# Start addresses of TensorE's operands at multiples of 64 bytes: a hybrid decoder trunk on one core

## The chip, the core and the metric

The kernel runs on one core of a Trainium2 chip. The metric is the device time of one launch in microseconds (us): the median of the kernel before is 1512.21 us over 3 runs (1512.15 to 1514.15).

## The reference

T = 272 tokens (16 learned ones ahead of 256) of D = 1024 features go through two layers in float32. Cut to what is computed:

```python
# layer 0
gate, xr = split(h @ w_in)                    # RG-LRU: 1024 -> 2 x 1344
xc = causal width-4 convolution of xr
r, i = sigmoid(blockdiag(xc) + b)             # 8 blocks of 168
a = exp(-8 r softplus(-lam)); u = sqrt(1 - a*a) * i * xc
hs = linear scan over time of (a, u)
h = LN(alpha h + (hs * gelu(gate)) @ w_out)
h = LN(alpha h + (silu(h @ wg) * (h @ wu)) @ w_ff_out)    # 1024 -> 3584 -> 1024
# layer 1
q, k, v, r, z = split(h @ w_in)               # gated linear attention, 4 heads, chunks of 64
h = LN(alpha h + (LN(attention) * silu(r)) @ w_out)
h = LN(alpha h + sum over the top 2 of 8 experts of gate * swiglu_e(h))   # 1024 -> 3584 -> 1024
out = h without the 16 learned tokens
```

## The kernel before

**Arithmetic.** Each large product is done in three passes of TensorE on operands of the type float32r. Weights and activations are split into a high part and a low part (`split`, line 269: a copy on ScalarE, a subtraction on VectorE), and `mm3` (line 273, matmuls at lines 275 to 277) issues low weight times high activation, high times low, high times high into one PSUM bank.

**Weights.** The class `Weights` streams all weights through SBUF: DMAs of up to 1 MB issued on SyncE's queue (line 97) into nine `raw` buffers (later up to 14), then pieces of 1024 columns split into `whi` on ScalarE (line 127) and `wlo` on VectorE (line 137), six buffers each. A piece is split four ahead of its use.

**Stages, in order of time.** In the trunk (all before the experts) a weight block of 128 x 128 is the stationary operand and one row of the tokens, `xh[:, k]` or `xl[:, k]`, is the moving one: 272 columns, 274 in a few stages (two more columns carry the norm's gain and bias), 256 or 258 where the learned tokens are left out. The stages are `xr` (convolution input, 264 matmuls), `g` (gates, 162), `gb` (gate branch, 264), `ro` (output of the recurrent block, 264), `fg`/`fu` (input of the dense channel mixer, 96 + 1248), `fo` (its output, 672), `z`/`k`/`q` (24 + 96 + 96), `vT` (192), `r` (192) and `go` (output of attention, 72 of 512 columns and 48 of 256). `xr`, `gb`, `fg`/`fu`, `z`, `k`, `q`, `vT` and `r` read `xh` and `xl`, 2472 matmuls in all. `g` and `ro` read `ch` and `cl`, `fo` reads `fh` and `fl`, whose rows are 272 elements apart. In `go` the roles are turned: `xh` and `xl` are stationary (128 columns of a row) and the weights move.

**Experts.** For each of 8 experts and 7 blocks j, `stage_in` (line 1319) does 48 matmuls with the gathered tokens `xe` stationary (128 x 128) and 512 weight columns moving, `stage_tr` (line 1337) transposes the gated product `hb` in four blocks and splits it into `hh` and `hl`, and `stage_out` (line 1351) does 24 matmuls with `hh` and `hl` stationary. That is 56 x 72 = 4032 matmuls of three passes, `pg`, `pu` and `y`.

**Places in SBUF.** Every tile takes a multiple of 32 bytes of each partition. Pools that live to the end lie one behind another from byte 1152 up: `wraw`, `wparts`, `const`, `keep`, `moe`, `late`, `rows`, `moe2`. Pools of the trunk are stacked from byte 229344 down (`side="right"`): `resid` (with `xh`, `xl`), below it `x`, and below that, one after another in time, `rg`, `ffn` and `gla`. A pool's tiles lie in the order of their creation from its lower end. So a tile of 32 bytes moves everything behind it in its own pool, and all pools stacked on that pool. In the allocation of the kernel before, the operands of the large products start here:

| tile | first byte | row pitch (bytes) | start mod 64 | start mod 128 |
|---|---|---|---|---|
| `whi`, `wlo` (all 12 buffers) | 74880 up | 512 or 2048 | 0 | 0 |
| `xh`: row k at 209504 + 1096 k | 209504 | 1096 | 32, 40, 48, 56, 0, 8, 16, 24 | 96, 40, 112, 56, 0, 72, 16, 88 |
| `xl` | 218272 | 1096 | the same | 32, 104, 48, 120, 64, 8, 80, 24 |
| `ch`; `cl` | 142048; 154016 | 1088 | 32 in every row | 96; 32, then alternating |
| `fh`; `fl` | 132160; 162624 | 1088 | 0 in every row | 64 in even rows, 0 in odd rows |
| `xe`, `hh`, `hl` (experts) | 213120 / 204928, 223360, 225408 | 512 | 0 | 0 |
| `x3h`, `x3l` (gathering) | 135648, 143840 | 512 | 32 | 96 |

**Order around the change.** The tokens' rows are written by `split` and by the class `Norm`; the edits touch the tiles alone. `clear` (line 696) fills 512 rows of `yd` in DRAM with zeros, four DMAs on SyncE's queue from the tile `zero`. `cm` (line 641) is a mask of 128 x 128 that GpSimd makes and VectorE copies into `cmask` at once; `tmp2` (lines 729 and 731) is a ring of two buffers for the exponents of the gates. The tiles of `moe`, `late` and `rows` lie where `gla` and `x` were, and each waits for the tiles that it overlaps.

Of the kernel before, what the change touches and what calls it, by code (L numbers as in the profile page):

```python
# [11 lines left out]
F32 = mybir.dt.float32  # L12
F32R = mybir.dt.float32r
# [6 lines left out]
P = 128  # L20
D = 1024
KD = D // P
NM = 16
NX = 256
T = NM + NX
ALPHA = float((2 * 2) ** 0.25)
EPS = 1e-5
TINY = 1e-34
# [157 lines left out]
def trunk_kernel(ctx: ExitStack, tc: tile.TileContext, xT_d, rgp_d, lnT_d, rgin_d, rgg_d, rgout_d,  # L186
                 fin_d, fout_d, bg_d, wup_d, zqk_d, vr_d, go_d, rows_d, rt_d, min_d, mout_d,
                 out, dbg=None):
    nc = tc.nc
# [44 lines left out]
    const = ctx.enter_context(tc.tile_pool(name="const", bufs=1))  # L234
    ps = ctx.enter_context(tc.tile_pool(name="ps", bufs=8, space=PSUM))
    dram = ctx.enter_context(tc.tile_pool(name="dram", bufs=1, space=bass.MemoryType.DRAM))
    yd = dram.tile([2 * NX + P, D], F32, name="yd")
# [15 lines left out]
    one_c = const.tile([P, 1], F32, name="one_c")  # L253
    nc.vector.memset(one_c, 1.0)

    onetri = const.tile([P, 2, P], F32, tag="onetri", name="onetri", bufs=1)
    ones, tri = onetri[:, 0], onetri[:, 1]
    nc.gpsimd.memset(ones, 1.0)
# [10 lines left out]
    def split(dst_h, dst_l, src):  # L269
        nc.scalar.copy(dst_h, src)  # L270
        nc.vector.tensor_sub(dst_l, src, dst_h)
# [6 lines left out]

    res = ExitStack()
    resid = res.enter_context(tc.tile_pool(name="resid", bufs=1, side="right"))  # L280
    xh = resid.tile([P, KD, T + 2], F32R, name="xh")
    xl = resid.tile([P, KD, T + 2], F32R, name="xl")
    nmu = resid.tile([P, T], F32, name="nmu")
    rstd_x = resid.tile([P, T], F32, name="rstd_x")
    lnT = resid.tile([P, 4, KD], F32, name="lnT")
    xs = ExitStack()
    x = xs.enter_context(tc.tile_pool(name="x", bufs=1, side="right")).tile([P, KD, T], F32, name="x")
    for n, (k0, k1) in enumerate(((0, 1), (1, 2), (2, 4), (4, 6), (6, 8))):
        W.limit = n + 1
        W.load()  # L290
        nc.sync.dma_start(x[:, k0:k1], xT_d[:, k0:k1])
        split(xh[:, k0:k1, :T], xl[:, k0:k1, :T], x[:, k0:k1])
    W.limit = len(units)
# [5 lines left out]
    def unfold(dst, pp, pool, name, c0=0):  # L299


        n = T - c0
        gb = pool.tile([P, 2], F32, tag="unfold", name=f"unfold_{name}", bufs=3)
        nc.vector.tensor_copy(gb, pp[:, n:n + 2])
        nc.vector.scalar_tensor_tensor(dst, nmu[:, c0:], gb[:, 0:1], pp[:, :n], op0=ALU.mult, op1=ALU.add)
        nc.vector.tensor_mul(dst, dst, rstd_x[:, c0:])
        return gb[:, 1:2]
# [8 lines left out]
    class Norm:  # L316
# [12 lines left out]
        def add(self, d, y):  # L329
            if d == 0:  # L330
                nc.vector.scalar_tensor_tensor(x[:, 0], x[:, 0], ALPHA, y, op0=ALU.mult, op1=ALU.add)
            else:
# [5 lines left out]
        def center(self):  # L338
# [6 lines left out]
            for k in range(1, KD):  # L345
                nc.vector.scalar_tensor_tensor(x[:, k], x[:, k], ALPHA, c, op0=ALU.mult, op1=ALU.subtract)
            self.square(0)
# [211 lines left out]
    def ffn_in(fs, c1):  # L559
        pps = [bank(f"f{t}{f}") for f in fs for t in "gu"]  # L560
        for k in range(KD):
            for pp in pps:
                mm3(pp[:, :c1], W.take(P), xk(k, 0, c1), k == 0, k == KD - 1)
            if c1 > T and k == 0:
                norm.sums(True)
        return pps
# [9 lines left out]
    fp = fps.enter_context(tc.tile_pool(name="ffn", bufs=1, side="right"))  # L576
    fh = fp.tile([P, NF, T], F32R, name="fh")
    fl = fp.tile([P, NF, T], F32R, name="fl")
    for f in range(NF):
        gt = fp.tile([P, T], F32, tag="gt", name=f"gt{f}", bufs=2)  # L580
        if f < 2:
            up = fp.tile([P, T], F32, tag="gt", name=f"up{f}", bufs=2)
            bg, bu = unfold(gt, first[2 * f], fp, f"fg{f}"), unfold(up, first[2 * f + 1], fp, f"fu{f}")
            nc.scalar.activation(gt, gt, AF.Silu, bias=bg)
            nc.vector.scalar_tensor_tensor(gt, up, bu, gt, op0=ALU.add, op1=ALU.mult)
        else:
            pg, pu = ffn_in((f,), T)
            silu = nc.scalar.activation(gt, pg[:, :T], AF.Silu)
            nc.vector.tensor_mul(gt, gt, pu[:, :T])
        split(fh[:, f], fl[:, f], gt)  # L590
# [47 lines left out]
    gp = ga.enter_context(tc.tile_pool(name="gla", bufs=1, side="right"))  # L638
    wu = gp.tile([P, 512], F32, tag="vm", name="wu", bufs=1)
    nc.sync.dma_start(wu, wup_d)  # L640
    cm = gp.tile([P, P], F32, name="cm")

    zero = gp.tile([P, 256], F32, name="zero")
    nc.gpsimd.memset(zero, 0.0)
    cmask = gp.tile([P, P], U32, name="cmask")
    nc.gpsimd.affine_select(out=cm, in_=ones, pattern=[[1, P]], compare_op=ALU.is_ge, fill=0.0, base=0,
# [47 lines left out]
    nc.gpsimd.memset(rstd_x, 0.0)  # L694

    def clear(a):
        nc.sync.dma_start(yd[a * P:(a + 1) * P].rearrange("p (b c) -> p b c", b=4),
                          zero[:, None, :].broadcast_to([P, 4, 256]))

    side.put([lambda: None] * 6 + [lambda g=g: gate_exp(g) for g in range(H)]  # L700
             + [lambda g=g: gate_log(g) for g in range(H)] + [lambda a=a: clear(a) for a in range(2 * NX // P)])
    for h in range(2, H):
        (pk,), (pq,) = qk((h,), T)
# [52 lines left out]
    def x_rows(i, q):  # L756
        pt = bank(f"xt{i}{q}")
        for k in range(4):
            nc.tensor.transpose(pt[:, k * P:(k + 1) * P], x[:, q * 4 + k, NM + i * P:NM + (i + 1) * P], ident)
        nc.scalar.activation(acc[:, i, q * 512:(q + 1) * 512], pt, AF.Copy, scale=ALPHA)  # L760

# [149 lines left out]
    moe = ctx.enter_context(tc.tile_pool(name="moe", bufs=1, reuse_waits="tile"))  # L911
    x3h = moe.tile([P, 2, D], F32R, name="x3h")
    x3l = moe.tile([P, 2, D], F32R, name="x3l")

    def small(name, shape, dt=F32):
        return moe.tile(shape, dt, name=name)
# [377 lines left out]
    def add_back(n, i):  # L1294
        a = acc[:, i]
        if n == 0:
            nc.vector.scalar_tensor_tensor(a, a, ALPHA, back[0][:, i], op0=ALU.mult, op1=ALU.add)
        else:
# [226 lines left out]
    with tc.If(nmax > P):  # L1525
# [3 lines left out]
        for e in range(NE):  # L1529
# [24 lines left out]
            for j in range(JM):  # L1554
                pg = bank(f"vpg{e}{j}")
                pu = bank(f"vpu{e}{j}")
                for kk in range(4):
                    w = raw_piece(min_d[e, j, kk // 2][:, (kk % 2) * PIECE:(kk % 2 + 1) * PIECE],
                                  f"vwi{e}{j}{kk}")
                    for k2 in range(2):  # L1560
                        k = kk * 2 + k2
                        for s, pp in ((0, pg), (1, pu)):
                            c = k2 * 1024 + s * 512
# [10 lines left out]
                for b, (q, s) in enumerate(out_blocks(e, j)):  # L1574
                    if b % 4 == 0:
                        w = raw_piece(mout_d[e, j][:, b * 512:(b + 4) * 512], f"vwo{e}{j}{b}")
                    c = b % 4 * 512
                    nc.tensor.matmul(py[s], ht[:, q * P:(q + 1) * P], w[:, c:c + 512],
                                     start=(j == 0 and q == 0), stop=(j == JM - 1 and q == 3))
            for s in range(2):  # L1580
                yv = gb.tile([P, 512], F32, tag="xg", name=f"vyv{e}{s}", bufs=4)
                nc.scalar.activation(yv, py[s], AF.Copy, scale=gs)
                for i in range(2):
                    c = slice(s * 512, (s + 1) * 512)
# [91 lines left out]
```

## Time and profile before

| | |
|---|---|
| median of 3 runs | 1512.21 us (1512.15 to 1514.15) |
| the profiled execution's own time | 1512.2 us |
| its span, first to last instruction | 1510.3 us |
| mean granted TensorE clock | 0.997 |
| TensorE busy | 1486.3 us, 98% |
| VectorE, ScalarE busy | 1262.3 us, 84%; 1058.7 us, 70% |

How to read it: TensorE's matmuls overlap, so the time that one takes (some 290 ns at 272 columns) is not the pace. The pace is the time from the start of one matmul to the start of the next, which the timeline gives to 10 ns, and to less over a run of many.

### The profile page before, as it was taken

Reading aid. Unit: us, or ns where it says so; the run is one execution under the profiler, and the core shown is the slowest. Engines: PE = TensorE matmul, PEld = TensorE weight load, DVE = VectorE, ACT = ScalarE, POOL = GpSimd, SP = SyncE. Lnnn points to the kernel's source line nnn. Section 1 sums busy time; section 2 is a strip of 40 time slices with the busy share of each in tenths; the row PEclk is TensorE's granted clock in tenths of the full one; section 3 lists DMA queues with packets and bytes.
Section 4 is the critical chain, followed back from the end, with each engine's and each line's share of the span. In section 5 each row is a group of like instructions: output and inputs, shape, how many; then the busy total and the mean of one; then the engine's idle time right before and its main releaser. Section 6 shows DMA issues by size and latency. Waiting matters only on the chain.

```text
span 1510.3 us, 22283 instructions
## 1 busy us (share of the span) xinstructions
PE 1486.3 (98%) x8393; PEld 1302.8 (86%) x8393; DVE 1262.3 (84%) x1492; ACT 1058.7 (70%) x1369; POOL 116.7 (8%) x151
## 2 busy tenths in 40 slices
PE   9989999999999999999999999999999999999996
PEld 9989999999998888888888888888888888888875
DVE  7699755555796699999998899898899899989897
ACT  6866644444685588878887778777787777777774
POOL 5443000002100000001000000000000000000001
PEclk9999999999999999999999999999999999999998
DMA  9536544445653579999999999999998899999973
GB/s 367 184 134 236 185 178 157 152 166 182 231 186 107 212 274 393 338 337 401 419 376 380 345 393 380 369 391 393 372 379 350 334 379 385 374 371 381 378 250 115
DMA packets 70500, 450.67 MB, mean 298 GB/s; under 512 B 8144, under 2 KB 10480, under 8 KB 22256
## 3 DMA queue, kind: packets, MB, share of 16 engines
q1 hardware_dynamic: 67696, 439.20, 76.7%
q0 software_dynamic: 2688, 9.96, 1.6%
q8 instruction: 68, 1.11, 0.3%
q14 instruction: 48, 0.39, 0.1%
HBM read 441.26 MB, written 7.86 MB: 297 GB/s over the span
## 4 chain that ended last, share of the span: by engine, by line
PE 92%; DVE 4%; ACT 2%; issue 1%; POOL 1%; DMA 0%; SPq 0%; DVEq 0%; ACTq 0%; POOLq 0%
PE pg L276 7%; PE pg L275 7%; PE pg L277 7%; PE y L276 7%; PE pu L276 7%; PE pu L277 7%; PE pu L275 7%; PE y L275 7%; PE y L277 7%; PE fg L276 2%; PE fg L277 2%; PE fu L275 2%; PE fo L275 2%; PE fo L276 2%; PE fo L277 2%; PE fg L275 2%
## 5 line engine op out<-in xcount | busy, mean ns | idle before, releaser
L137 DVE TENSOR_TENSOR wlo<-raw,whi 128x1024 fp32r<-128x1024 f32 (+1 forms) x839 | 979.9, 1214 | 131.6 <-ACT whi L127 125.3
L127 ACT CAST whi<-raw 128x1024 fp32r<-128x1024 f32 (+1 forms) x841 | 834.1, 1039 | 154.5 <-PE fu L277 43.5
L276 PE MATMUL pg<-wlo,xe 128*128 128x512 f32 x448 | 178.2, 398 | 0.1
L275 PE MATMUL pg<-whi,xe 128*128 128x512 f32 x448 | 177.4, 396 | 0.7 <-DVE xe L1061 0.7
L276 PE MATMUL y<-wlo,hh 128*128 128x512 f32 (+1 forms) x452 | 175.8, 389 | 0.6 <-DVE wlo L137 0.5
L277 PE MATMUL y<-whi,hh 128*128 128x512 f32 (+1 forms) x452 | 175.1, 387 | 0.0
L277 PE MATMUL pg<-whi,xe 128*128 128x512 f32 x448 | 175.0, 391 | 0.0
L276 PE MATMUL pu<-wlo,xe 128*128 128x512 f32 x448 | 174.8, 390 | 0.0
L277 PE MATMUL pu<-whi,xe 128*128 128x512 f32 x448 | 174.8, 390 | 0.0
L275 PE MATMUL pu<-whi,xe 128*128 128x512 f32 x448 | 174.6, 390 | 0.0
L275 PE MATMUL y<-whi,hl 128*128 128x512 f32 (+1 forms) x452 | 151.4, 388 | 0.4 <-DVE yl L1395 0.4
L1333 ACT ACTIVATE hb<-pg 128x512 f32<-128x512 f32 x56 | 33.3, 595 | 127.6 <-PE pg L277 127.6
L276 PEld LDWEIGHTS y<-wlo,hh 128*128 128x128 f32 x452 | 84.9, 188 | 19.9 <-DVE wlo L137 2.8
L275 PEld LDWEIGHTS y<-whi,hl 128*128 128x128 f32 x452 | 84.9, 188 | 18.2 <-DVE yl L1395 0.9
L276 PEld LDWEIGHTS pu<-wlo,xe 128*128 128x128 f32 x448 | 84.1, 188 | 18.1
L277 PEld LDWEIGHTS y<-whi,hh 128*128 128x128 f32 x452 | 84.8, 188 | 17.2
L277 PEld LDWEIGHTS pu<-whi,xe 128*128 128x128 f32 x448 | 84.1, 188 | 18.0
L275 PEld LDWEIGHTS pu<-whi,xe 128*128 128x128 f32 x448 | 84.1, 188 | 17.7
L275 PEld LDWEIGHTS pg<-whi,xe 128*128 128x128 f32 x448 | 84.2, 188 | 17.5 <-DVE xe L1061 0.9
L276 PEld LDWEIGHTS pg<-wlo,xe 128*128 128x128 f32 x448 | 84.3, 188 | 16.4 <-DVE wlo L137 1.1
L277 PEld LDWEIGHTS pg<-whi,xe 128*128 128x128 f32 x448 | 84.3, 188 | 16.0
L1334 DVE TENSOR_TENSOR hb<-hb,pu 128x512 f32<-128x512 f32 x56 | 38.3, 684 | 42.3 <-ACT hb L1333 39.4
(444 smaller groups left out, 2626.1 us busy)
## 6 DMA issues: line engine op xcount, KB each, us to landing
raw<-min SPq DMA_DIRECT2D x216, 1024.0 KB, 7.3
raw<-mout SPq DMA_DIRECT2D x106, 1024.0 KB, 7.6
raw<-fin SPq DMA_DIRECT2D x28, 1024.0 KB, 4.6
raw<-fout SPq DMA_DIRECT2D x16, 896.0 KB, 4.4
raw<-vr SPq DMA_DIRECT2D x8, 1024.0 KB, 4.8
raw<-min SPq DMA_DIRECT2D x16, 512.0 KB, 6.0
raw<-rgin SPq DMA_DIRECT2D x7, 1024.0 KB, 16.9
raw<-rgout SPq DMA_DIRECT2D x8, 704.0 KB, 3.9
```

Of the source, the lines that this page charges most:

```text
L127: self.high[i] = nc.scalar.copy(hi[:, :n], src).ins
L137: self.last_low = low.tensor_sub(lw[:, :n], src, hi[:, :n]).ins
L275: nc.tensor.matmul(out_ap, w[1], xr[0], start=start, stop=False, skip_group_check=skip)
L276: nc.tensor.matmul(out_ap, w[0], xr[1], start=False, stop=False, skip_group_check=skip)
L277: nc.tensor.matmul(out_ap, w[0], xr[0], start=False, stop=stop, skip_group_check=skip)
L1333: behind(W.coming(n, 2), lambda: nc.scalar.activation(hb, pg, AF.Silu))
L1334: nc.vector.tensor_mul(hb, hb, pu)
```

## The change

The rows of `xh` and `xl` are made 288 elements (1152 bytes) apart, of which 274 are used. A tile of 8 elements (32 bytes) that nothing reads or writes is added to the pools `const`, `resid`, `ffn` and `moe`. To make room, `cm` uses a buffer of the ring `tmp2`, and `zero` is 128 columns wide in place of 256, so `clear` reads it eight times over in place of four. `T` and all instructions on data are otherwise as they were.

```diff
+ROW = 288
...
+    const.tile([P, 8], F32, name="even")
     onetri = const.tile([P, 2, P], F32, tag="onetri", name="onetri", bufs=1)
...
-    xh = resid.tile([P, KD, T + 2], F32R, name="xh")
-    xl = resid.tile([P, KD, T + 2], F32R, name="xl")
+    xh = resid.tile([P, KD, ROW], F32R, name="xh")[:, :, :T + 2]
+    xl = resid.tile([P, KD, ROW], F32R, name="xl")[:, :, :T + 2]
...
+    resid.tile([P, 8], F32, name="even_r")
...
     fl = fp.tile([P, NF, T], F32R, name="fl")
+    fp.tile([P, 8], F32, name="even_f")
...
-    cm = gp.tile([P, P], F32, name="cm")
-
-    zero = gp.tile([P, 256], F32, name="zero")
+    cm = gp.tile([P, P], F32, tag="tmp2", name="cm", bufs=2)
+
+    zero = gp.tile([P, P], F32, name="zero")
...
-        nc.sync.dma_start(yd[a * P:(a + 1) * P].rearrange("p (b c) -> p b c", b=4),
-                          zero[:, None, :].broadcast_to([P, 4, 256]))
+        nc.sync.dma_start(yd[a * P:(a + 1) * P].rearrange("p (b c) -> p b c", b=D // P),
+                          zero[:, None, :].broadcast_to([P, D // P, P]))
...
     x3l = moe.tile([P, 2, D], F32R, name="x3l")
+    moe.tile([P, 8], F32, name="even_m")
```

## Rows read from the trace of the kernel before

**Rows 1.** The page: the engines' busy time, and the chain that ended last.
```profile
PE 1486.3 (98%) x8393; PEld 1302.8 (86%) x8393; DVE 1262.3 (84%) x1492; ACT 1058.7 (70%) x1369; POOL 116.7 (8%) x151
...
PE 92%; DVE 4%; ACT 2%; issue 1%; POOL 1%; DMA 0%; SPq 0%; DVEq 0%; ACTq 0%; POOLq 0%
```

**Rows 2.** Windows: stretch, length, engines busy (instructions), granted clock, DMA share, GB/s.
```profile
139.50:310.40 170.90, 170.90 (x1350) 170.38 (x1349) 105.46 (x148) 85.65 (x135) 0.00 (x0) 1.00 0.48 171
...
396.50:426.00 29.50, 29.50 (x230) 28.93 (x229) 28.49 (x57) 25.51 (x47) 3.84 (x18) 1.00 0.69 240
...
535.80:1492.00 956.20, 955.47 (x4361) 789.04 (x4361) 877.15 (x868) 739.87 (x836) 26.68 (x18) 1.00 0.94 363
```

**Rows 3.** Timeline of TensorE in fg/fu: start, duration; first matmul of rows k.
```profile
298.29 0.29 PE L275 MATMUL fg<-xh,wlo 128*128 128x272 f32 x1
...
299.04 0.29 PE L275 MATMUL fg<-xh,wlo 128*128 128x272 f32 x1
...
299.81 0.29 PE L275 MATMUL fg<-xh,wlo 128*128 128x272 f32 x1
...
300.56 0.29 PE L275 MATMUL fg<-xh,wlo 128*128 128x272 f32 x1
...
301.32 0.28 PE L275 MATMUL fg<-xh,wlo 128*128 128x272 f32 x1
...
304.35 0.29 PE L275 MATMUL fg<-xh,wlo 128*128 128x272 f32 x1
```

**Rows 4.** The same view in fo: first matmul of successive rows f.
```profile
338.84 0.29 PE L275 MATMUL fo<-fh,wlo 128*128 128x272 f32 x1
...
339.21 0.29 PE L275 MATMUL fo<-fh,wlo 128*128 128x272 f32 x1
...
339.59 0.29 PE L275 MATMUL fo<-fh,wlo 128*128 128x272 f32 x1
...
339.97 0.29 PE L275 MATMUL fo<-fh,wlo 128*128 128x272 f32 x1
...
340.35 0.29 PE L275 MATMUL fo<-fh,wlo 128*128 128x272 f32 x1
...
342.62 0.29 PE L275 MATMUL fo<-fh,wlo 128*128 128x272 f32 x1
```

**Rows 5.** The same view in ro: first and last of an unbroken run of 48.
```profile
125.02 0.29 PE L276 MATMUL ro<-cl,whi 128*128 128x272 f32 x1
...
130.93 0.29 PE L275 MATMUL ro<-ch,wlo 128*128 128x272 f32 x1
```

**Rows 6.** The same view in the experts: transposes, then 12 and 59 matmuls.
```profile
567.93 0.60 PE L1341 MATMUL pt<-ident,hb 128*128 128x128 f32 x4
...
568.60 0.40 PE L276 MATMUL pg<-wlo,xe 128*128 128x512 f32 x1
...
571.14 0.39 PE L275 MATMUL pg<-whi,xe 128*128 128x512 f32 x1
...
584.29 0.39 PE L276 MATMUL pu<-wlo,xe 128*128 128x512 f32 x1
```

**Rows 7.** The same view in go: first and last of an unbroken run of 24.
```profile
510.69 0.40 PE L275 MATMUL go<-whi,xl 128*128 128x512 f32 x1
...
516.07 0.39 PE L277 MATMUL go<-whi,xh 128*128 128x512 f32 x1
```

**Rows 8.** Groups by line: transposes from hb (start 0 mod 64) and vt (32).
```profile
L1341 PE MATMUL pt<-ident,hb 128*128 128x128 f32 x224 | 33.8, 272 | 0.0
...
L753 PE MATMUL vt<-ident,vt 128*128 128x128 f32 x24 | 3.3, 272 | 0.0
```

**Rows 9.** Timeline of SyncE's queue: the zero fill and the weight loads around it.
```profile
402.51 3.73 SPq L697 DMA_DIRECT2D yd<-zero  x4
409.27 0.34 SPq L97 DMA_DIRECT2D raw<-vr  x1
```

## The prediction

> **What bounds the kernel now.** I read the busy times and the chain first: TensorE is busy 98% of the span and carries 92% of the chain that ended last [rows 1]. [...] So the time is the pace of the matmuls, and the question is what an operand's start does to it. The pace stands in the timeline, from start to start. [...]
>
> **Places after the change**, worked out from the table of starts. `resid` becomes 2 x 9216 + 2 x 1088 + 128 + 32 = 20768 bytes, so `xh` starts at 229344 - 20768 = 208576 and `xl` at 217792; both are 64 mod 128, and at a pitch of 1152 = 9 x 128 so is every row. `x` starts at 199872; `ffn` gets 32 bytes and starts at 131200: `fh` and `fl` are 0 in even rows and 64 in odd ones, before the other way round. `ch` comes to 64 mod 128 and `cl` to 0, alternating with the row. From `const` on, the left side moves up 32 bytes (`x3h` and `x3l` come to 0), and from behind `x3l` on 64 bytes: `xe`, `hh` and `hl`, which stood at 0 mod 128, now stand at 64. `whi` and `wlo` stay at 0. So the 4032 matmuls of the experts and the 672 of `fo` had multiples of 64 before. What is new is `xh`, `xl`, `ch`, `cl`, the gathering and the small products of attention, and, as a side effect, the other half of 128 bytes in the experts.
>
> **The 2472 matmuls on xh and xl.** Rows k of `xh` start at 96, 40, 112, 56 mod 128. Rows 0 and 2, at multiples of 16, take 0.75 us each for six matmuls, 125.0 ns; rows 1 and 3, 8 bytes off such a multiple, take 0.77 and 0.76 us, 127.5 ns [rows 3]. What does a row at 64 mod 128 take? The nearest are the even rows of `fo`, which start there with the same weights: 0.37 + 0.38 us for six, 125.0 ns, against 0.38 + 0.38, 126.7 ns, for the odd rows at 0 [rows 4]. The whole run of 30 in `fo` is at (342.62 - 338.84) / 30 = 126.0 ns although every row there is a multiple of 64. I take 125.0 ns: 2184 matmuls of 272 or 274 columns x 1.2 ns = 2.6 us less. [...] The 288 of 256 or 258 columns (`q`, `r`) I leave as they are; a nanosecond either way is 0.3 us.
>
> [...]
>
> **go.** Here `xh` and `xl` are stationary and the weights move, 512 columns. A run of 24 goes at (516.07 - 510.69) / 23 = 233.9 ns [rows 7], the experts at 226.7. After the change the stationary starts are all alike, as in the experts; 72 x 7.2 = 0.5 us at most, and nothing if the cause is another. I take 0.4 us, and the 48 of 256 columns at nothing.
>
> **g and ro** (426 matmuls) go from 32 and 96 mod 128, at (130.93 - 125.02) / 47 = 125.7 ns [rows 5], to 0 and 64, as `fo` at 126.0: 0.1 to 0.2 us more. `fo` itself only swaps its halves: nothing, at most 672 x 0.5 = 0.3 us either way.
>
> **Experts.** 4032 matmuls, whose stationary operand moves from 0 to 64 mod 128. I take nothing, since after the transposes the pace always comes back to 226.7 ns, but the price is high: 1 ns is 4.0 us. Bounds are the rivals below.
>
> **The rest.** Transposes from a start of 32 (`vt`) and from 0 (`hb`) take 272 ns alike [rows 8]: nothing for attention's small products. `clear` moves the same bytes in pieces of 512 in place of 1024, twice the number; its four DMAs hold SyncE's queue 3.73 us, and the next weight load behind them is issued at 409.27, after 3.0 us of slack [rows 9]. Doubled, they would delay it by 0.7 us, for weights that `vT` uses from 426 us on; TensorE has no gap in that stretch [rows 2]. If that cover were gone it would cost that 0.7 us. `cm` in the ring is copied out long before an exponent takes its buffer, and `zero` is cleared in half the time on an idle GpSimd. Of the tiles behind `moe`, the buffer `xeC` now overlaps `rbs`, whose last reader, the router's bias product, comes before the last blocks of `go`, after which alone the loads into `late` can start: no wait is longer. The 32-byte tiles issue nothing.
>
> **Sum.** -2.6 - 0.4 + 0.2 = -2.8 us on the profiled execution's 1512.2 us (a span of 1510.3 and 1.9 around it), which is also the median: 1509.4 us.
>
> **Rivals.**
> A, the forecast: 1509.4 us, by its bounds 1508.1 to 1511.0. Chance 0.45. About 0.2%, 3.0 us, is the least that a measurement can tell from no change, so of this some 0.20 is faster and 0.25 is no change.
>
> B, slower: the experts don't settle. Just after the four transposes 12 matmuls go at (571.14 - 568.60) / 11 = 230.9 ns, and only then at 226.7 [rows 6]; `go`, whose stationary starts vary from row to row, never settles in 24 and stays at 233.9 [rows 7]. If with stationary rows at 64 and moving rows at 0 mod 128 the settled pace is not found, 4032 x 4.2 to 7.2 ns = 17 to 29 us are lost: 1526 to 1538. If it is found later, twice the 11 x 4.2 ns per block, it is 56 x 0.046 = 2.6 us. It decides from a mean loss of 0.7 ns per matmul, where it eats up A. For it: `go`. Against: in the experts the starts are alike among themselves, before and after. Chance 0.19, all but 0.02 slower.
>
> C, faster than A: in `fo`, the moving rows that lie in the other half of 128 bytes than the stationary ones are 1.7 ns quicker than those in the same half [rows 4]. After the change that holds in the experts too: 4032 x 1.7 = 6.9 us more, 1502.5. Against: it rests on times read to 10 ns, and a settled pace may not care. Chance 0.14.
>
> [...] Chance 0.18, no change.
>
> [...] Chance 0.04. [...]
>
> **How the numbers follow.** Predicted is A's 1509.4. Faster: 0.20 + 0.14 + 0.04 = 0.38; within 0.2%: 0.25 + 0.18 + 0.02 = 0.45; slower: 0.17. The range 1501 to 1520 leaves out E, half of C below, and the dear half of B above, about 0.2. A's own range is 1508.1 to 1511.0.
>
> **What would show it.** In `fg`/`fu` the eight rows k should take equal times, near 0.75 us for six matmuls, and 6.00 us for 48. `go` should come to 227 to 230 ns. In the experts the run after a block's transposes should again come to 226.7 ns within about 12 matmuls: 230 or more there is B, 225 is C. `vT` must start without a gap. The forecast is wrong if the experts' window differs by more than 3 us from 956.2, or if the trunk up to 498 us gains more than 4 us or loses any.

## The result and the profile after

The changed kernel takes 1535.09 us (median of 4 runs, 1532.9 to 1535.87), the one before in the same session 1512.86 us (4 runs): a ratio of 1.0144, 95% interval 1.0126 to 1.0161. It is 22 us slower, where 2.8 us faster was forecast; the time lies in rival B's range (1526 to 1538) and outside the range given. Runs of one kernel fall on two levels 2 to 3 us apart (before: near 1512.2 and near 1514), so smaller differences are read below from profiled spans and lowest runs.

The profiled execution of the changed kernel took 1535.87 us, of which 1534.0 are the span; before, 1512.2 and 1510.3. The busy times and the chain still name TensorE, with two points less of the chain [rows 1]:

```profile
PE 1510.3 (98%) x8393; PEld 1305.9 (85%) x8393; DVE 1263.5 (82%) x1492; ACT 1060.2 (69%) x1369; POOL 122.3 (8%) x151
...
PE 90%; DVE 5%; ACT 2%; issue 1%; POOL 1%; DMA 0%; SPq 0%; DVEq 0%; ACTq 0%; POOLq 0%
```

The windows of the changed kernel tell where the time went [rows 2]: `fg`/`fu`, a stretch ahead of the experts that rows 2 don't have, and the experts from their first matmul to 18.3 us before the span's end, as in rows 2.

```profile
139.50:309.00 169.50, 169.26 (x1349) 168.73 (x1348) 105.44 (x148) 85.39 (x135) 0.00 (x0) 1.00 0.48 172
526.50:533.00 6.50, 6.50 (x33) 6.50 (x32) 2.22 (x12) 3.33 (x6) 0.00 (x0) 0.50 0.51 166
537.00:1515.70 978.70, 978.06 (x4362) 790.38 (x4362) 878.51 (x869) 741.64 (x836) 25.13 (x18) 1.00 0.93 355
```

The same 4362 instructions of the experts (4361 before) take 978.7 us in place of 956.2: 22.5 us more, at a granted clock of 1.00 and with TensorE busy throughout. So the matmuls themselves are slower. The balance of the spans: the gathering `xg` starts at 525.6 us in place of 527.4 (the trunk gained 1.8); from there to the first `pg` pass 11.4 us in place of 8.4 (3.0 lost, in the middle row above: a granted clock of 0.50 from 526.5 to 533.0); the experts lose 22.5. That is -1.8 + 3.0 + 22.5 = 23.7 us, the whole of 1534.0 - 1510.3.

The timeline of the changed kernel in the experts shows the pace: the transposes, the matmuls after them, and a run as long as that of [rows 6].

```profile
569.72 0.60 PE L1347 MATMUL pt<-ident,hb 128*128 128x128 f32 x4
...
570.40 0.39 PE L278 MATMUL pg<-wlo,xe 128*128 128x512 f32 x1
...
573.19 0.40 PE L278 MATMUL pg<-wlo,xe 128*128 128x512 f32 x1
...
586.73 0.40 PE L279 MATMUL pu<-whi,xe 128*128 128x512 f32 x1
```

From 573.19 to 586.73 lie 58 steps, 13.54 / 58 = 233.4 ns, where the same number took 226.7. The start times to the nanosecond alternate between steps of 231 and 236 ns, mean 233.3. That is 6.6 ns above the 226.7 of before. The pace no longer comes down after the transposes: the first steps (570.40 to 573.19, 12 steps of 232.5) are within 1 ns of all the rest.

In `fg`/`fu` the same view shows what was forecast [rows 3]: first matmuls of rows k, and the one 48 matmuls after the first.

```profile
297.04 0.29 PE L277 MATMUL fg<-xh,wlo 128*128 128x272 f32 x1
...
297.80 0.29 PE L277 MATMUL fg<-xh,wlo 128*128 128x272 f32 x1
...
298.54 0.29 PE L277 MATMUL fg<-xh,wlo 128*128 128x272 f32 x1
...
299.30 0.29 PE L277 MATMUL fg<-xh,wlo 128*128 128x272 f32 x1
...
303.04 0.29 PE L277 MATMUL fg<-xh,wlo 128*128 128x272 f32 x1
```

48 matmuls take 6.00 us, 125.0 ns each, against 6.06. But the rows are not alike: they take 0.76 and 0.74 us by turns, so "the eight rows take equal times" was wrong.

In `go` the run of 24 [rows 7] goes at (514.23 - 508.90) / 23 = 231.7 ns, not at 227 to 230:

```profile
508.90 0.39 PE L277 MATMUL go<-whi,xl 128*128 128x512 f32 x1
...
514.23 0.40 PE L279 MATMUL go<-whi,xh 128*128 128x512 f32 x1
```

And SyncE's queue [rows 9] holds the zero fill for 4.44 us in place of 3.73. The slack ahead of the next load falls from 3.0 us to 407.89 - 401.20 - 4.44 = 2.25, the load is issued 1.4 us earlier than before, as the whole stage is, and TensorE is busy for 28.00 of 28.00 us from 396.5 to 424.5: that cover held.

```profile
401.20 4.44 SPq L702 DMA_DIRECT2D yd<-zero  x4
407.89 0.34 SPq L98 DMA_DIRECT2D raw<-vr  x1
```

### The profile page after: what moved, and what is told of

The parts are those of the page before. It is cut to its first block, busy times and chain, and to the rows that moved or that the text cites. A ratio compares the mean times of both kernels' runs of the same rounds, so it can differ in the third digit from the quotient of the medians.

```text
span 1534.0 us, 22283 instructions
## 1 busy us (share of the span) xinstructions
PE 1510.3 (98%) x8393; PEld 1305.9 (85%) x8393; DVE 1263.5 (82%) x1492; ACT 1060.2 (69%) x1369; POOL 122.3 (8%) x151
## 4 chain that ended last, share of the span: by engine, by line
PE 90%; DVE 5%; ACT 2%; issue 1%; POOL 1%; DMA 0%; SPq 0%; DVEq 0%; ACTq 0%; POOLq 0%
PE pu L277 7%; PE pu L279 7%; PE y L279 7%; PE pg L278 7%; PE y L277 7%; PE pg L279 7%; PE pg L277 7%; PE y L278 7%; PE pu L278 7%; DVE wlo L138 2%; PE fo L277 2%; PE fo L279 2%; PE fo L278 2%; PE fu L279 2%; PE fg L277 2%; PE fg L279 2%
## 5 line engine op out<-in xcount | busy, mean ns | idle before, releaser
L277 PE MATMUL pg<-whi,xe 128*128 128x512 f32 x448 | 179.2, 400 | 0.7 <-DVE xe L1067 0.7
L279 PE MATMUL y<-whi,hh 128*128 128x512 f32 (+1 forms) x452 | 178.4, 395 | 0.0
L277 PE MATMUL pu<-whi,xe 128*128 128x512 f32 x448 | 178.0, 397 | 0.0
L279 PE MATMUL pu<-whi,xe 128*128 128x512 f32 x448 | 178.0, 397 | 0.0
L279 PE MATMUL pg<-whi,xe 128*128 128x512 f32 x448 | 177.2, 396 | 0.0
```

The source lines that it names most:

```text
L277: nc.tensor.matmul(out_ap, w[1], xr[0], start=start, stop=False, skip_group_check=skip)
L279: nc.tensor.matmul(out_ap, w[0], xr[0], start=False, stop=stop, skip_group_check=skip)
```

## The experiments

The question was which place counts: the absolute start of the stationary operand, or its start against that of the moving one, and with what period. Below, "distance" is the stationary start less the moving start, in bytes mod 256. It comes out of the table of starts: before, `whi`, `wlo`, `xe`, `hh` and `hl` all stand at 128 mod 256, distance 0 in the experts. The change moved `xe`, `hh` and `hl` by 64: distance 64.

### The 64 bytes alone

The kernel before, with an empty piece of 64 bytes behind `x3l`: all else stays where it was.

```diff
     x3l = moe.tile([P, 2, D], F32R, name="x3l")
+    moe.tile([P, 16], F32, name="half")
```

> The kernel before with nothing but an empty tile of 64 bytes behind x3l, so that xe, hh and hl start at 64 mod 128; the trunk is untouched. Theory R: the experts settle at 233.2 ns, 1512.5 + 26 = 1536 to 1540 us. Theory M: 1512 to 1514 us.

Measured: 1535.93 us, ratio 1.0147 (1.0126 to 1.0169). The whole loss comes from these 64 bytes, as theory R had it and theory M had not. The timeline shows the pace of the changed kernel, 60 steps in 14.00 us, 233.3 ns:

```profile
570.66 0.60 PE L1342 MATMUL pt<-ident,hb 128*128 128x128 f32 x4
...
573.43 0.39 PE L276 MATMUL pu<-wlo,xe 128*128 128x512 f32 x1
...
587.43 0.39 PE L276 MATMUL pu<-wlo,xe 128*128 128x512 f32 x1
```

### Both operands moved by 64

The kernel before, with the same piece ahead of `whi` and `wlo`, so that both operands of the experts stand at 64 mod 128.

```diff
+    parts.tile([P, 16], F32, name="half", bufs=1)
```

> The kernel before with an empty tile of 64 bytes ahead of whi and wlo: the weights and xe, hh and hl all start at 64 mod 128. Theory R (relative): moving and stationary agree again, the experts stay at 226.7 ns and the total at 1510 to 1516 us (the trunk's rows meet weights at 64, which may move it by 2 us either way). Rival theory Z (absolute: only a stationary start at 0 mod 128 is read at the good pace): 233 ns and 1536 us or more.

Measured: 1513.66 us, ratio 0.9999 (0.9989 to 1.001). The experts are back, 50 steps in 11.34 us, 226.8 ns:

```profile
576.71 0.39 PE L276 MATMUL pg<-whi,xe 128*128 128x512 f32 x1
...
588.05 0.39 PE L278 MATMUL pg<-whi,xe 128*128 128x512 f32 x1
```

So a start at 64 mod 128 is not slow by itself (theory Z): with both operands there the experts are as fast as with both at 0. What the 64 bytes alone changed is the distance.

### 128 bytes on

The changed kernel, with the piece behind `x3l` at 96 bytes: `xe`, `hh` and `hl` are multiples of 128 again, at distance 128.

```diff
-    moe.tile([P, 8], F32, name="even_m")
+    moe.tile([P, 24], F32, name="even_m")
```

> The change, with the empty tile in the pool moe 64 bytes longer, so that xe, hh and hl start at 0 mod 128 again as in the kernel before; all else as in the change. Theory R (what counts is where the stationary rows start against the moving ones, within 128 bytes): the experts come back from 233.2 to 226.7 ns per matmul, 4032 x 6.5 = 26 us less than the change, and the trunk keeps its gain of 1 to 2 us: 1509 to 1512 us. Theory M (the loss comes from something else in the change: the entry into the experts at the lower clock, the zero fill, the memory that pools share): 1530 us or more.

Measured: 1530.86 us, ratio 1.0123 (1.0105 to 1.0141). In the experts 48 steps take 11.20 us, 233.3 ns:

```profile
569.55 0.40 PE L277 MATMUL pg<-whi,xe 128*128 128x512 f32 x1
...
580.75 0.40 PE L277 MATMUL pg<-whi,xe 128*128 128x512 f32 x1
```

The period of 128 bytes fell; it had to be longer, or the starts counted otherwise. The time is the one of theory M, but not its cause: the 64 bytes alone lose as much, without the rest of the change.

### One distance for each expert

The kernel of the last experiment, with `xe` of each expert pushed further by its own number of bytes in a wider tile. The offsets in the expectation are counted from that kernel's place, which is distance 128 itself and not 0. The odd experts' buffer starts there; the even experts' buffer lies behind it, and the 128 bytes by which the tile is wider bring it to distance 0. So the distance is the offset for even experts, and 128 more for odd ones.

```diff
-        t = m2.tile([P, 2, KD, P], F32R, tag=("xeA", "xeB")[e % 2], name=f"xe{e}", bufs=1)
+        t = m2.tile([P, 2 * D + 32], F32R, tag=("xeA", "xeB")[e % 2], name=f"xe{e}", bufs=1)
+        c = (0, 8, 4, 16, 12, 24, 28, 32)[e]
+        t = t[:, c:c + 2 * D].rearrange("p (s k t) -> p s k t", s=2, k=KD)
```

> As e1_back_to_0, but the tokens of each expert start at another place against the moving weights: experts 0 to 7 at 0, 32, 16, 64, 48, 96, 112 and 128 bytes; hh and hl stay at 0. One look at the pace of pg and pu, expert by expert. Theory R: 226.7 ns at 0 and 128, 233.2 at 64, other values between or beyond at the rest. A rival, that only agreement counts: 233 at every place but 0 and 128. [...]

Measured in a single run: 1528.41 us. Mean step of `pg` and `pu` (transients included), from the start times of 336 matmuls of each expert:

```
expert     0      7      2      3      1      4      5      6     (y, all)
distance   0      0      16     192    160    48     224    112    128
ns         228.1  228.2  230.0  229.4  233.3  233.2  233.1  233.2  232.8
```

Distance 0 mod 256 is the fast one, in two experts far apart in time; 192 lies between, and the others but 16 lose all. A period of 128 would have made 128 as good as 0, and if the place mod 16 bytes alone counted, all would be as good. The 230.0 of distance 16 is not a pace of its own but a mean of two, as the timeline of one block of expert 2 shows (48 matmuls into the same two PSUM tiles, with the transposes between):

```profile
791.98 0.40 PE L277 MATMUL pg<-whi,xe 128*128 128x512 f32 x1
...
795.95 0.39 PE L279 MATMUL pu<-whi,xe 128*128 128x512 f32 x1
796.18 0.60 PE L1349 MATMUL pt<-ident,hb 128*128 128x128 f32 x4
...
796.85 0.39 PE L278 MATMUL pg<-wlo,xe 128*128 128x512 f32 x1
...
803.20 0.40 PE L279 MATMUL pu<-whi,xe 128*128 128x512 f32 x1
```

Straight behind `y` 17 steps take 3.97 us, 233.5 ns; behind the transposes 28 steps take 6.35 us, 226.8 ns. The distance is 16 in both, so what ran before decides which of the two paces is found. In expert 0, at distance 0, both stretches settle at 226.6 to 226.8.

### 256 bytes on: the changed kernel, repaired

The changed kernel with 224 bytes behind `x3l`: distance 0 again at another absolute place.

```diff
-    moe.tile([P, 8], F32, name="even_m")
+    moe.tile([P, 56], F32, name="even_m")
```

> The changed kernel with the empty piece behind x3l at 224 bytes in place of 32, so that xe, hh and hl stand 256 bytes behind where they stood before the change: stationary start less moving start is 0 mod 256 again in the experts, at another absolute place than before. Theory of 256 (the pace hangs on stationary start less moving start mod 256 bytes): the experts settle at 226.7 ns, surplus 32 cycles, and the trunk keeps what it gained, so 1509 to 1512 us, faster than before by 1.5 to 3 us at most, with the lost dip of the clock at the experts' entry or without. Rival (more than 256, or only the old place will do): 233 ns and 1530 to 1536 us.

Measured: 1512.51 us, ratio 0.9995 (0.9985 to 1.0004), just above the 1509 to 1512 expected and far from the rival's. The experts settle, 50 steps in 11.34 us, 226.8 ns (no run shows the cycles of the expectation, only times). Their window is that of before; the stretch ahead of them is at full clock in this execution:

```profile
526.50:533.00 6.50, 5.59 (x46) 5.21 (x44) 4.42 (x18) 4.05 (x8) 0.00 (x0) 1.00 0.39 150
533.10:1489.20 956.10, 955.27 (x4361) 789.10 (x4361) 877.11 (x868) 739.95 (x836) 26.91 (x18) 1.00 0.95 363
```

```profile
570.05 0.39 PE L278 MATMUL pg<-wlo,xe 128*128 128x512 f32 x1
...
581.39 0.39 PE L277 MATMUL pu<-whi,xe 128*128 128x512 f32 x1
```

A shift by 256 brings the pace back, where 128 did not. The profiled span is 1507.5 us, 2.8 less than before, and the lowest run is 2.2 us below the lowest of before (1509.24 and 1511.48); by the ratio it is not told apart from no change. A fall of the granted clock like that of the changed kernel ahead of the experts, 3.0 us, is as large as this gain: it stands in four of the nine profiles of whole kernels (the change, the 64 bytes alone, both moved, one distance for each expert), and not in those of before and of this kernel.

### A map of distances

A small kernel of its own: runs of 36 matmuls back to back, each with its own weights, the moving start fixed and the stationary start s bytes further.

```python
for i in range(36):
    m, s = seq[i % len(seq)]
    nc.tensor.matmul(b[:, :cols], st[:, (i % 4) * P + s // 4:(i % 4) * P + s // 4 + P],
                     mv[:, (i % 2) * D + m // 4:(i % 2) * D + m // 4 + cols], start=True, stop=True)
```

> Not the computation of the reference: runs of 36 matmuls back to back, each with its own weights, and the input copied to the output; only the pace of each run is read. In each run the moving start is fixed and the stationary start is s bytes further mod 256, s = 0 to 240 in steps of 16; then two groups of 272 columns whose moving start changes from matmul to matmul. Theory of 256: 512 columns at s = 0 take 226.7 ns and at other places more, up to 233.3; 256 columns are lowest near s = 64 (113.5 ns) and 120 at s = 0; 272 columns have places at or below 125.0 ns and places at 126.7 or above, and not the same places as 512. Rival (the pace comes from the pattern of the kernel, as from its PSUM banks or its evictions, and not from the starts): one pace over all s in each group, within 1 ns.

Measured: mean ns of the last 23 steps of each run:

```
distance        0      16     32     48     64     80     96     112
512 columns   226.7  226.7  233.4  233.3  233.2  232.1  234.5  233.4
272 columns   125.1  124.9  126.7  126.7  123.3  126.6  123.4  126.7
256 columns   120.0  118.1  118.4  117.7  113.3  118.7  118.8  120.2
distance       128    144    160    176    192    208    224    240
512 columns   233.5  233.4  233.4  229.7  228.9  233.3  233.3  226.7
272 columns   126.6  123.3  126.6  126.7  126.7  125.8  125.7  125.0
256 columns   118.8  118.3  120.2  118.0  117.8  116.7  116.8  119.9
```

The timeline joins matmuls of one form; here are pieces of the runs at 512 columns and distances 0 and 64, and at 272 columns and distances 64 and 192 (start, length, count):

```profile
12.71 5.83 PE L41 MATMUL b<-mv,st 128*128 128x512 f32 x25
...
45.90 5.99 PE L41 MATMUL b<-mv,st 128*128 128x512 f32 x25
...
162.59 3.74 PE L41 MATMUL b<-mv,st 128*128 128x272 f32 x29
...
199.10 3.46 PE L41 MATMUL b<-mv,st 128*128 128x272 f32 x26
```

Less one matmul's own 0.39 us, the first piece has 24 steps of 226.7 ns and the second 24 of 233; less 0.29, the third has 28 steps of 123.2 and the fourth 25 of 126.8. So the starts alone are enough to change the pace, without the kernel's evictions, DMAs or accumulation. The map also gives the trunk's 125.0 ns: with rows 1152 bytes apart the distance is 192 in the even rows of `xh` and `xl` and 64 in the odd ones, and (123.3 + 126.7) / 2 = 125.0, as the 0.74 and 0.76 us of `fg`/`fu` say. And a run with the moving rows of `fo` (three matmuls at each of four places 64 apart) takes 126.09 ns; `fo` itself takes 126.09. Eight more runs of 272 columns, with the moving start 8 bytes further, took 123.3 to 128.9 ns, so a start 8 bytes off a multiple of 16 is not dear by itself either. Of the numbers of columns tried, 512 are quickest at distance 0, 272 at 64, 96 and 144, and 256 at 64.

### Which matmul's starts?

The same small kernel, with two matmuls by turns.

```python
for d in (128, 64, 96):
    run(512, [(0, 0), (d, d)])     # each matmul's own starts agree
    run(512, [(0, d), (d, 0)])     # the next one's stationary start agrees
```

> Not the computation of the reference: runs of 36 matmuls back to back, the input copied to the output; only paces are read. Which two starts must agree? In runs of two matmuls by turns, (moving, stationary) = (0, 0), (d, d): each matmul's own starts agree, and the stationary start of the next matmul stands d from the moving start of the one that runs. In (0, d), (d, 0) it is the other way round. Theory of the load beside (the weights of the next matmul are read from SBUF while the moving rows of this one are, and the two readers meet or miss each other by their places mod 256): for d = 128 and 96 at 512 columns the first order goes at 233.3 ns and the second at 226.7; 272 and 256 columns with 64 and 192 likewise (123.3 and 126.7; 113.3 and 118 or more). Rival (own starts: the bits of one instruction count): the first order 226.7, the second 233.3. Rival (absolute places): both orders the same. Both starts at 128: 226.7 by either of the first two. [...] The same weights throughout: if they are loaded again each time, the paces stay 226.7 and 233.3 at 0 and 128.

Measured, the pair of d = 128 in the timeline, and then distance 16 held:

```profile
45.24 6.10 PE L41 MATMUL b<-mv,st 128*128 128x512 f32 x26
...
53.48 6.14 PE L41 MATMUL b<-mv,st 128*128 128x512 f32 x26
...
120.87 6.23 PE L41 MATMUL b<-mv,st 128*128 128x512 f32 x26
```

Less 0.39 us each has 25 steps: 228.4 ns with own starts agreeing, 230.0 with the next one's, and 233.6 at distance 16. Over the last 23 steps the pairs took 228.2 and 230.0 (d = 128), 231.9 and 231.6 (64), 233.8 and 229.7 (96). With 64 and 192 both orders took 123.3 ns at 272 columns and 116.6 to 116.7 at 256, where 113.3 or 118 had been expected. All starts at 0, and all at 128, took 226.65; (0, 128) throughout 233.5. Neither theory wins: at d = 128 either agreement helps and neither is enough, and at 96 own starts that agree don't help at all. The edges of the map don't hold either: distance 16, at 226.7 in the map, took 233.35 here, distance 240, at 226.7 in the map, took 228.3, and distance 228 took 226.65. Only distance 0 settled at 226.7 wherever it was held. Away from it the pace also hangs on what ran before, as the block of expert 2 showed. The same weights throughout took 226.70 and 232.3 at 0 and 128.

So the pace of back-to-back matmuls changes with the places of the two operands, from 226.65 ns (all starts at 0) to 233.5 ((0, 128) throughout). Whether it is the reading of the two that meets, no run here shows.

### A layout from the map

The repaired kernel, with the rows of `xh` and `xl` by turns in one tile, a pair every 2304 bytes (9 x 256), so that each stage holds one distance for `xh` and one for `xl`, and `fh`, `fl` at 32 mod 64.

```diff
-    xh = resid.tile([P, KD, ROW], F32R, name="xh")[:, :, :T + 2]
-    xl = resid.tile([P, KD, ROW], F32R, name="xl")[:, :, :T + 2]
+    xhl = resid.tile([P, KD, 2 * ROW], F32R, name="xhl")
+    xh, xl = xhl[:, :, 4:T + 6], xhl[:, :, T + 8:2 * T + 10]
...
-    resid.tile([P, 8], F32, name="even_r")
+    resid.tile([P, 36], F32, name="even_r")
...
-    fp.tile([P, 8], F32, name="even_f")
+    fp.tile([P, 12], F32, name="even_f")
```

> The kernel with the experts' operands 256 bytes on, and xh and xl rows by turns in one tile, a pair every 2304 bytes (9 x 256), so that the stationary start stands 48 bytes behind every row of xh and 224 behind every row of xl, mod 256; fh and fl moved so that their four places are 160, 96, 32 and 224. The computation is the whole one. Theory of 256 with the map of the small kernel: runs of the order xh, xl, xh at these places took 122.96 ns in the small kernel, so the 2184 trunk matmuls go from 126.2 to about 123.0 ns (7.0 us less than before), fo from 126.0 to 125.0 (0.7 us less), the experts stay at 226.7: 1504 to 1506 us, about 7 us less than before and 5 less than the same kernel with rows 1152 bytes apart. Rival (the trunk's pace doesn't follow the map, the 125.0 ns of the changed kernel came from multiples of 64 bytes): 80 and 160 are no multiples of 64, so 126 ns or more and 1511 to 1514 us.

The second differs in the place alone (`even_r` of 60 elements, `even_f` of 56):

> The same but with all of xh and xl 96 bytes lower: the stationary start 144 bytes behind the rows of xh and 64 behind those of xl. Theory of 256 with the map of the order xh, xl, xh: this place took 126.83 ns in the small kernel, so the trunk loses against the run beside it 2184 x 3.9 ns = 8.5 us: 1512 to 1515 us. Rival (each matmul has its own price by its own place, whatever its neighbours' are): alone, 144 and 64 both took 123.3 ns, so as fast as the run beside it, 1504 to 1507 us. Rival (the places don't matter): the same time as beside it.

Measured: 1508.94 us, ratio 0.9975 (0.9966 to 0.9985), and 1511.04 us, ratio 0.998 (0.9971 to 0.999). Both beat the kernel before and the changed one; lowest runs 1508.37 and 1507.99 against 1511.72, profiled spans 1506.8 and 1506.3 against 1510.3 before and 1507.5 for the repaired kernel. Of the first, both expected ranges missed (1504 to 1506 and 1511 to 1514): about half of the 7 us came. Of the second the forecast of 1512 to 1515 missed, and the rival that it is like the run beside it fits the spans. In `fg`/`fu` 48 matmuls take 5.97 us in either; the rows of the first:

```profile
290.35 0.29 PE L277 MATMUL fg<-xhl,wlo 128*128 128x272 f32 x1
...
296.32 0.29 PE L277 MATMUL fg<-xhl,wlo 128*128 128x272 f32 x1
```

That is 124.4 ns, better than the 125.0 of the changed kernel, at 80 and 160 mod 256, which are no multiples of 64. But the map of mixed distances had said 122.96 and 126.83 for these two places, 8.5 us apart, and they are alike: it doesn't carry over from the small kernel. The 122.96 was no settled pace there: the first 12 steps of that run took 125.3 ns, the last 12 122.3. In the second, `fg` and `fu` settle apart at the same distances (125.8 and 123.1 ns). `fo` went from 126.1 to 125.3 ns, close to what the map has for its new places (125.0 to 125.2).

## Why the prediction was wrong

**The step that failed** is the one on the experts: "I take nothing, since after the transposes the pace always comes back to 226.7 ns." It came back where the two starts agreed mod 256, and the change took just that away: the settled pace of 4032 matmuls went from 226.7 to 233.3 ns, and their window grew by 22.5 us, 5.6 ns each (the first dozen behind the transposes had been slower before, too). The price was in the text, as rival B's 17 to 29 us, but at a chance of 0.19, and that was brought down by a wrong reason: "in the experts the starts are alike among themselves, before and after." All stationary starts are alike, but what counts is how they stand to the moving ones, as the move of both by 64 shows. The rows had a hint: the long runs at 226.7 ns are those where all starts agree mod 256 [rows 6], and `go`, where 512 columns move past stationary starts that, but for one row of `xh`, don't, stays at 233.9 [rows 7]. The prediction read `go` as unlike among itself; `go` after the change, at distances 64 and 192, stays at 231.7.

**The trunk** was right in the pace of `fg`/`fu`: 126.2 (6.06 us for 48 in [rows 3]) to 125.0 ns on the rows named, 6.00 us for 48 as written beforehand. On the profiled spans the repaired kernel, which is the forecast with the experts left in peace, gains 2.8 us, the number of the sum, but a part of that is luck. The first matmul of `g` and the first of the gathering tell it, first in the kernel before, then in the repaired one:

```profile
41.69 0.29 PE L275 MATMUL g<-ch,wlo 128*128 128x272 f32 x1
...
527.40 0.40 PE L952 MATMUL xg<-sel,x3h 128*128 128x256 f32 x2
```

```profile
40.64 0.29 PE L277 MATMUL g<-ch,wlo 128*128 128x272 f32 x1
...
524.71 0.41 PE L958 MATMUL xg<-sel,x3h 128*128 128x256 f32 x2
```

From `g` on the trunk takes 485.7 and 484.1 us, 1.6 less; the changed kernel gains 1.8 there. The other 1.05 us lie ahead of `g`, where 264 matmuls at 1.2 ns account for 0.3: the kernel with the 64 bytes alone, whose trunk is that of before, also reaches `g` at 40.73. Less what `go` gained and `g` and `ro` lost (below), the matmuls on `xh` and `xl` behind `xr` gained 1.9 us, where 1920 x 1.2 = 2.3 was forecast. The reason was wrong too: 64 bytes are no bound, and 125.0 is the mean of a good distance and a bad one (123.3 and 126.7 in the map).

**go** was forecast at 227 to 230 ns and 0.4 us less; it came to 231.7, 72 x 2.2 = 0.16 us. **g and ro** lost 0.4 us in the repaired kernel's profile, 0.25 in the changed one's, where 0.1 to 0.2 was forecast. **fo** stayed at 126.1, with its halves swapped (even rows from 125.1 to 127.4 ns, odd rows from 127.1 to 124.8), and the **zero fill** (4.44 us on SyncE's queue) and **transposes** (272 ns from `hb`, 273 from `vt`, where both were 272) cost nothing, as forecast. Clearing `zero` took 0.204 us in place of 0.312, which is not half. The upper end of A's own range, 1511.0, follows from no term. The lower end, 1508.1, would need 3.9 us from the 2184 matmuls, 1.8 ns each, which no run with rows 1152 bytes apart shows: `fg`/`fu` gained 1.2 there.

**The rivals.** B came true in mechanism and size: with the two starts 64 bytes apart the settled pace is not found. That the place mod 16 bytes alone counts, as the 2.5 ns between the rows of [rows 3] could suggest, is out as well: by it the shift of 64 bytes could do nothing, and distances 64 and 192 would be alike at 272 columns (123.3 and 126.7). C (1.7 ns quicker in the other half of 128 bytes) went the other way: at distance 64 the experts are 6.6 ns slower, so what `fo` shows at 272 columns says nothing of 512. No change, at a chance of 0.18, was half right: 64 bytes are no bound (124.4 ns at 80 and 160 mod 256), but `fg`/`fu` gained 1.2 ns and the experts lost 6.6. E, which the range left out, did not come: the lowest pace at 272 columns with one distance held is 123.26 ns, 2.9 below the 126.2 of before.

**What stays open** is why equal starts mod 256 give the quicker pace, why the best distance changes with the number of columns, and what the pace keeps from the matmuls before.

## What to carry to other kernels

When a kernel lives on back-to-back matmuls with a weight load each, look at the distance between the stationary and the moving start mod 256 bytes, not at either's alignment: at 512 columns of float32r, as here, give both the same start mod 256 (226.7 ns, against 233.3 at distances 64 and 128). A best place for other shapes has to be measured in the kernel itself, since the map of the small kernel did not carry over. An empty piece in a pool is an edit of everything stacked behind it, so list which operands change their distance to their partner before costing it at nothing. A pace that "always comes back" is a state with a cause; price the edit by whether the cause survives it.

## What the runs showed of the hardware

- 512 columns of float32r with a weight load each: settled at 226.65 ns at distance 0 mod 256 wherever it was held, near 233.3 at most others.
- 272 columns, one distance held in the small kernel: 123.3 ns at 64, 96 and 144, 126.7 at most others; 256 columns: 113.3 at 64, 120.0 at 0.
- The pace at some distances depends on what ran before: at distance 16 one block of an expert went at 233.5 ns behind `y` and at 226.8 behind the transposes; the two small kernels held 226.7 and 233.35.
- The granted clock fell ahead of the experts in four of the nine profiles of whole kernels (to 0.50 from 526.5 to 533.0 us in the changed kernel's); from 520 to 526 us, ahead of the fall, TensorE was busy 5.31 of 6 us in the changed kernel, where it fell, and 5.35 in the kernel before, where it didn't.
